# Experts of a two-layer block stack: the tokens' shift added on the vector engine, the gather issued a quad ahead, another order of the quads

## The chip, the core and the metric

The kernel runs on one core of one Trainium2 chip. A time is the device time of one execution in microseconds (us); of several runs the median is given. Its engines have their own instruction queues and run side by side: TensorE (PE; its weight loads are shown as PEld), the vector engine (DVE), ScalarE (ACT), GpSimd (POOL), and SyncE (SP), which here only issues transfers (DMA). Results of matmuls land in PSUM, all other tiles lie in SBUF.

## What is computed

A sequence of 256 tokens and a context of 256 tokens, each token a row of 1024 numbers, go through two layers and a few blocks behind them. Each layer has a mixer (attention and a convolution or pooling) and a mixture of 32 experts. Its input is normalised, then scaled and shifted by vectors that depend on the stream (one pair for the sequence, one for the context):

```python
h = _rmsnorm(x, gain) * (1 + scale) + shift        # scale, shift: one row of 1024 a stream

def _moe(h, grp_w, grp_b, exp_w, exp_b, w_gate, w_up, w_down):
    ...                      # a group of experts for each token, 2 experts in it, their weights
    def run(args):
        tok, wt, e = args
        xb = h_pad[tok]
        hid = jax.nn.silu(xb @ w_gate[e]) * (xb @ w_up[e])
        return (hid @ w_down[e]) * wt[:, None]
    ...                      # each token's two results are added up
```

A layer's experts hold 32 x 3 matrices of 1024 x 512 numbers in fp32, 201 MB. Layer 0 takes 512 tokens (both streams), layer 1 only the sequence's 256.

## The kernel before

The program runs eight stages one after the other: ab, moe0, cd, moe1 (the two layers), ar, mlp0, moba, mlp1. The change touches `moe`, which runs for layer 0 (four tiles of 128 tokens, two streams) and for layer 1 (two tiles, one stream).

**Weights.** The experts lie in eight quads of four. A quad has six units: two of gate weights, two of up, two of down. A unit is four transfers of 1024 KB on SP's queue (`experts`). Units go into a ring of three slots in layer 0 and four in layer 1, in the order in which they are used; `s.done(...)` behind a unit's last matmul frees its slot, and the next unit is issued into it. Each quad has a fixed number of blocks of 128 places for tokens, `BLOCKS`: in layer 0 quad 0 has two, quad 1 three, quads 2 to 4 two, quads 5 to 7 one; in layer 1 quad 1 has two and the others one. The quads run in the order `ORDER`, [0, 6, 1, 2, 3, 4, 5, 7].

**A quad.** `gather` builds a one-hot matrix OH (tokens by places) on the vector engine (L1150, L1151) and multiplies it with the tokens' rows, kept without their shift in two parts (mH, mL), so that the tokens of the quad stand in hg, transposed (L1533, L1534: 64 matmuls in layer 0, into banks of the PSUM tag `tp`, of which there are two). The shift comes in by a further product: four matmuls count for each place which stream it takes (L1528; ScalarE copies the result to `cnt`, L1529), and eight matmuls of four rows multiply that with the shift vectors (L1537). ScalarE copies a full bank to hg (L1539). The shift's rows are made earlier, by `shift_rows` within the router's stage: ScalarE copies at L1214 and L1215, vector engine at L1218. `quad` then multiplies hg with the gate and up units (L1570), 32 matmuls a unit and block; OH is transposed (L1579) and copied by ScalarE to OT (L1580); ScalarE takes silu of the gate part (L1584), the vector engine the product with the up part (L1585), TensorE transposes that (L1588), the vector engine copies it to hidT (L1589), and the down units follow (L1598). `split` cuts the result into two parts (ACT L1609, DVE L1610), and `add` multiplies them with OT, which brings them back to the tokens' rows (L1619, L1620; DVE L1622 and GpSimd L1624 add them to xs). The two halves of a quad's `add` are issued within the next quad, behind its first and its second gate unit.

**The order of the work.** Only the matmuls of a unit are kept in program order; what stands around them on TensorE is placed by a scheduler. The gathers of the second to sixth quad stand between the quad before and their own gate units, with pieces within the down units of the quad before.

**The general part.** Tokens that don't fit into a quad's blocks are handled by `leftover`, a branch and a loop that runs as many times as there are such groups; for these inputs it runs zero times. It stands behind the first `PART` = 6 quads. Ahead of it the last quad's `add` is done at once (the flush), behind it the remaining quads 5 and 7 run, gather first.

**Router weights.** Layer 1's (tile rtw, transfer issued by ScalarE in `router`, L1182) share a buffer with `cnt`, so they are fetched when cnt was used for the last time in layer 0, in quad 7.

Of the kernel before, what the change touches and what calls it, by code (L numbers as in the profile page):

```python
# [10 lines left out]
F32 = mybir.dt.float32  # L11
F32R = mybir.dt.float32r
# [3 lines left out]
OP = mybir.AluOpType  # L16
# [217 lines left out]
class K:  # L234
# [86 lines left out]
    def setup(s):  # L321
# [41 lines left out]

        s.sel = cp.tile([128, 2, 4, 4], F32, name="sel")
        ids = s.ident.rearrange("p (i c) -> p i c", i=4)
        for l in range(2):
            for o in (0, 2):
                nc.vector.tensor_copy(s.sel[:, l, :, o:o + 2], ids[:, :, 12 * l + 2:12 * l + 4])
        s.low = cp.tile([128, 1], F32, name="low")
        for o in (0, 64):  # L370
            nc.vector.tensor_scalar(s.low[o:o + 32], s.ip[:32, 0:1], 2.0, -1.0, op0=OP.is_ge, op1=OP.mult)
        s.ones = cp.tile([128, 128], F32, name="ones")
        nc.vector.memset(s.ones, 1.0)
        nc.vector.tensor_scalar(nsk, sk, -1.0, None, op0=OP.mult)
# [825 lines left out]
    def shift_rows(s, l, pool, pp):  # L1200


        nc, V = s.nc, s.nc.vector
        ps = pp.tile([128, 512], F32, name="sc", tag="sc", bufs=2)
        for i in range(4):
            o = 64 * (i // 2)
            nc.tensor.matmul(ps[o:o + 4, i % 2 * 256:(i % 2 + 1) * 256], s.sel[:, l, i], s.mods[1], start=True,
                             stop=True, skip_group_check=True)
        yield
        w = pool.tile([128, 512], F32, name="sw", tag="hw", bufs=4)  # L1210
        H = pool.tile([128, 512], F32R, name="swH", bufs=1)
        rows = [slice(o, o + 4) for o in (0, 64)]
        for o in rows:
            nc.scalar.activation(w[o], ps[o], AF.Copy)  # L1214
            nc.scalar.activation(H[o], ps[o], AF.Copy)  # L1215
        yield
        for o in rows:
            V.scalar_tensor_tensor(s.shift[o], H[o].bitcast(F32), s.low[o], w[o], op0=OP.mult, op1=OP.add)  # L1218

    def moe(s, l, tiles):  # L1220
# [4 lines left out]
        with ExitStack() as ctx:  # L1225
# [6 lines left out]
            s.shift = big.tile([68, 512], F32R, name="shift")  # L1232
# [5 lines left out]
            with tc.tile_pool(reuse_waits="tile", name="me_rt", bufs=3) as rp:  # L1238
# [6 lines left out]

                tk = rp.tile([128, 70], F32, name="tk", bufs=1)
                nc.gpsimd.memset(tk, 0.0)
                for o in (1, 3, 65, 67):
                    nc.gpsimd.memset(tk[:, o:o + 1], 1.0)
                s.take = big.tile([128, 70], F32R, name="take")  # L1250
                nc.gpsimd.tensor_copy(s.take, tk)

# [66 lines left out]
                with tc.manual_schedule(engines={mybir.EngineType.PE, mybir.EngineType.DVE}):  # L1319
                    shift = s.shift_rows(l, rp, pp)  # L1320
                    if nt > 2:
                        turn(0)
                        next(shift)
# [6 lines left out]
                        next(shift)  # L1330
                        square(3, False)
                        next(shift, None)
                    else:
                        next(shift)
                        next(shift)
# [3 lines left out]
                        next(shift, None)  # L1339
# [18 lines left out]
            base = np.cumsum([0] + blocks) * 128.0  # L1358

            for part in (range(s.PART), range(s.PART, 8)):  # L1360
                with tc.tile_pool(reuse_waits="tile", name="me_wk", bufs=1) as wk:
                    if part[0] == 0:
                        before = (rest, lambda: (s.table(pp, lx, s.ltab), s.slot_weights(nt, wk, pp, slot, wk_, wcol)))
                    for i in part:
                        q = s.ORDER[i]
                        got = first if i == 0 else s.gather(tiles, blocks[q], float(base[q]), qk, pp, hH, hL, slot)
                        split, add = s.quad(l, q, nt, blocks[q], int(base[q]), tiles, wk, qk, pp, g2, wcol, got, before)
                        tag = "tp" if i < 7 and max(blocks[q], blocks[s.ORDER[i + 1]]) > 2 else "sc"
                        before = (lambda: (add(0, tag), split(1)), lambda: add(1, tag))
                    if part[0] == 0:  # L1370
                        for f in before:
                            f()
                        before = (lambda: None,) * 2
                    else:
                        split(1)
                        for t in sorted(range(nt), key=lambda t: t < nt - 2):
                            for n in range(2):
                                add(n, ("tp", "sc")[n], (t,), True)
                if part[0] == 0:
                    with tc.tile_pool(reuse_waits="tile", name="me_lo", bufs=1) as wk:  # L1380
                        s.leftover(l, nt, tiles, wk, pp, hH, hL, g2, slot, wk_)
# [8 lines left out]
    PART = 6  # L1390
    ORDER = [0, 6, 1, 2, 3, 4, 5, 7]

    def leftover(s, l, nt, tiles, wk, pp, hH, hL, g2, slot, wt):
# [7 lines left out]
        with tc.If(n > 0), tc.For_i(0, n, 1) as it:  # L1401
# [27 lines left out]
            for t in range(nt):  # L1429
                o = 1 - tiles[t] // 2  # L1430
                mm(ps[:4, :32], s.take[:, o:o + 4].bitcast(F32), OH[:, t], start=t == 0, stop=t == nt - 1)
            cnt = wk.tile([4, 32], F32, name="lcnt")
            V.tensor_copy(cnt, ps[:4, :32])

            sh = wk.tile([4, 512], F32, name="lsh", tag="t", bufs=1)
# [967 lines left out]
```

## Time and profile before

| what | value |
|---|---|
| three runs | 2330.93 us median (2329.2 to 2331.31) |
| the profiled execution | 2333.8 us, its span 2331.8 us |
| TensorE busy in the span | 2060.5 us (88%) |
| vector engine, ScalarE, GpSimd busy | 1132.4, 796.7, 299.9 us |
| read from memory | 597 MB, 256 GB/s over the span |
| layer 0's experts | first gate matmul at 338.5, last scatter at 881.7 us |
| layer 1's experts | from about 1035 to about 1486 us |

Matmuls are pipelined: each lasts longer than the distance to the next, so the cost of a series is its busy time over its count or the distance between its first and last start. [...] "Idle before" a row is the time in which its engine did nothing ahead of it, and behind the arrow stands what ended that time.

### The profile page before, as it was taken

Reading aid. Unit: us, or ns where it says so; the run is one execution under the profiler, and the core shown is the slowest. Engines: PE = TensorE matmul, PEld = TensorE weight load, DVE = VectorE, ACT = ScalarE, POOL = GpSimd, SP = SyncE. Lnnn points to the kernel's source line nnn. Section 1 sums busy time; section 2 is a strip of 40 time slices with the busy share of each in tenths; the row PEclk is TensorE's granted clock in tenths of the full one; section 3 lists DMA queues with packets and bytes.
Section 4 is the critical chain, followed back from the end, with each engine's and each line's share of the span. In section 5 each row is a group of like instructions: output and inputs, shape, how many; then the busy total and the mean of one; then the engine's idle time right before and its main releaser. Section 6 shows DMA issues by size and latency. Waiting matters only on the chain. (4 is left out here: it accounts for less than half of the span.)

```text
span 2331.8 us, 33216 instructions
## 1 busy us (share of the span) xinstructions
PE 2060.5 (88%) x12749; PEld 1300.4 (56%) x12749; DVE 1132.4 (49%) x2315; ACT 796.7 (34%) x1595; POOL 299.9 (13%) x292
## 2 busy tenths in 40 slices
PE   5987989999998778988887776789999999999998
PEld 3763754434443336553322232587967887777886
DVE  4897582202222018561110111478857666877666
ACT  4353441101110006630000000365325555655555
POOL 1000020201102012010000000242101110021110
PEclk8998989999998799998998979897999999999999
DMA  9775519987998794359999999840024455434550
GB/s 347 298 289 172 189 55 398 423 340 309 378 376 356 298 392 183 127 220 424 424 424 425 424 392 424 358 163 10 1 109 177 153 190 196 152 118 167 190 189 36
DMA packets 95125, 600.34 MB, mean 257 GB/s; under 512 B 12912, under 2 KB 14064, under 8 KB 30448
## 3 DMA queue, kind: packets, MB, share of 16 engines
q1 hardware_dynamic: 88848, 589.34, 63.8%
q10 hardware_dynamic: 6112, 8.80, 1.1%
q8 instruction: 104, 1.70, 0.3%
q14 instruction: 61, 0.50, 0.1%
HBM read 597.05 MB, written 1.05 MB: 256 GB/s over the span
## 5 line engine op out<-in xcount | busy, mean ns | idle before, releaser
L414 DVE TENSOR_TENSOR L<-w,H 128x512 fp32r<-128x512 f32 (+1 forms) x520 | 368.3, 722 | 188.7 <-ACT H L413 178.7
L1570 PE MATMUL acc<-w,hg 128*32 128x512 f32 x2816 | 389.1, 618 | 49.9 <-DMA w<-exw 48.7
L413 ACT ACTIVATE H<-w 128x512 fp32r<-128x512 f32 (+1 forms) x528 | 324.6, 621 | 308.4 <-PE hid L1694 75.2
L1570 PEld LDWEIGHTS acc<-w,hg 128*32 128x32 f32 x2816 | 100.8, 113 | 292.6 <-issue 200.9
L1598 PE MATMUL acc<-w,hidT 128*32 128x512 f32 x1408 | 215.9, 642 | 49.9 <-DMA w<-exw 43.2
L1624 POOL TENSOR_TENSOR xs<-xs,yo 128x512 f32<-128x512 f32 x90 | 114.5, 1301 | 814.3 <-DVE yo L1622 814.0
L1694 PE MATMUL hid<-mh,H 128*128 128x512 f32 x512 | 185.1, 404 | 6.7 <-DVE mh L1643 5.4
L1585 DVE TENSOR_TENSOR sg<-acc,sg 128x512 f32<-128x512 f32 x22 | 15.2, 692 | 355.2 <-PE acc L1570 355.0
L1609 ACT ACTIVATE yH<-acc,kept 128x512 fp32r<-128x512 f32 x44 | 30.1, 688 | 418.5 <-PE acc L1598 359.8
L1610 DVE SCALAR_TENSOR_TENSOR yL<-acc,kept,yH 128x512 fp32r<-128x512 f32 x44 | 33.0, 749 | 279.6 <-ACT yH L1609 278.4
L1598 PEld LDWEIGHTS acc<-w,hidT 128*32 128x32 f32 x1408 | 51.6, 116 | 190.9 <-issue 99.9
L1695 PE MATMUL hid<-mh,L 128*128 128x256 f32 x512 | 145.2, 284 | 0.5 <-DVE L L414 0.5
L1533 PE MATMUL tp<-OH,mH 128*128 128x128 f32 (+2 forms) x384 | 111.2, 319 | 28.8 <-DVE OH L1151 12.3
L1694 PEld LDWEIGHTS hid<-mh,H 128*128 128x128 f32 x512 | 97.6, 191 | 32.8 <-ACT H L413 4.4
L1622 DVE TENSOR_TENSOR yo<-sc,g 128x512 f32<-128x512 f32 x74 | 49.6, 688 | 133.2 <-PE sc L1620 131.5
L1534 PE MATMUL tp<-OH,mL 128*128 128x128 f32 (+2 forms) x384 | 108.6, 311 | 0.0
L1533 PEld LDWEIGHTS tp<-OH,mH 128*128 128x128 f32 x384 | 82.9, 216 | 43.9 <-issue 29.1
L423 PE MATMUL pd<-L,uH 128*128 128x512 f32 x256 | 102.5, 400 | 1.1 <-DVE L L414 0.2
L1704 POOL TENSOR_TENSOR uL<-r,uH 128x256 fp32r<-128x256 f32 x64 | 59.2, 952 | 342.0 <-ACT uH L1703 254.8
L422 PE MATMUL pd<-H,uH 128*128 128x512 f32 x256 | 101.2, 395 | 0.0
L424 PE MATMUL pd<-H,uL 128*128 128x512 f32 x256 | 101.2, 395 | 0.0
L1695 PEld LDWEIGHTS hid<-mh,L 128*128 128x128 f32 x512 | 98.2, 192 | 1.6 <-DVE L L414 1.1
(716 smaller groups left out, 3898.6 us busy)
## 6 DMA issues: line engine op xcount, KB each, us to landing
w<-exw SPq DMA_DIRECT2D x384, 1024.0 KB, 16.4
w<-modw SPq DMA_DIRECT2D x96, 512.0 KB, 7.1
w<-up SPq DMA_DIRECT2D x32, 1024.0 KB, 4.9
w<-dn SPq DMA_DIRECT2D x32, 1024.0 KB, 4.7
w<-qkv SPq DMA_DIRECT2D x12, 1024.0 KB, 4.8
w<-pg SPq DMA_DIRECT2D x8, 1024.0 KB, 4.8
w<-ab_u SPq DMA_DIRECT2D x4, 1024.0 KB, 13.6
w<-ab_o SPq DMA_DIRECT2D x4, 1024.0 KB, 4.8
```

The lines of the kernel that those rows point to most:

```text
L413: nc.scalar.activation(H, w, AF.Copy)
L414: (nc.gpsimd if k % 8 in s.spread else nc.vector).tensor_sub(L, w, H.bitcast(F32))
L422: mm(o, a[0], b[0], start=start, stop=False)
L423: mm(o, a[0], b[1], start=False, stop=False)
L424: mm(o, a[1], b[0], start=False, stop=stop)
L1533: mm(got[k][1], hH[:, t, c], OH[:, t], start=t == 0 and k % n == 0, stop=False, skip_group_check=True)
L1534: mm(got[k][1], hL[:, t, c], OH[:, t], start=False, stop=False, skip_group_check=True)
L1570: mm(pg[m, a][32 * i:32 * i + 32, :], hg[:, 4 * hf + k, c:c + 32], u[:, i, k], start=hf == 0 and k == 0, stop=hf == 1 and k == 3, skip_gro ...
L1598: mm(py[n, a][32 * i:32 * i + 32, :], hT[:, a, 2 * hf + k, 32 * i:32 * i + 32], u[:, i, k, n * 512:(n + 1) * 512], start=hf == 0 and k == ...
L1624: (V if last and n else nc.gpsimd).tensor_add(xv, xv, tmp)
L1694: nc.tensor.matmul(ps[m], H[:, w], h[:, k], start=k == 0, stop=False, skip_group_check=True)
L1695: nc.tensor.matmul(ps[m][:, :256], L[:, w], h[:, k, :256], start=False, stop=k == 7, skip_group_check=True)
```

## The change

`shift_rows`, the count and the shift matmuls go. Instead `of_stream` multiplies a matrix of ones with OH, two matmuls for each stream, so that every partition has, for each place, how often the stream's tokens fill it; ScalarE copies that to `rows`. `shifted` then adds shift x rows to the gathered bank on the vector engine, once for each stream and 128 features: 16 instructions a gather in layer 0, which write hg. In layer 1, with one stream, ScalarE writes hg with the shift as a bias, eight instructions a gather. The next quad's `gather` is issued by the running one (`ahead`), between its up units and the transposes of its hid part; the whole loop over quads is in program order on TensorE; OT's transposes move ahead of the up units; hid is copied back into its own tile. `ORDER` becomes [0, 5, 1, 6, 2, 3, 4, 7] and `PART` 7, so that the general part's branch stands ahead of the last quad alone. The transfer of the router weights no longer waits for `cnt`.

```diff
+    def of_stream(s, pool, pp, tiles, OH, W, tag):
+        streams = sorted({t // 2 for t in tiles})
+        if len(streams) == 1:
+            return None
+        rows = pool.tile([128, 2, W], F32, name="rows", bufs=1)
+        one = s.ones if OH.dtype == F32 else s.onesr
+        for st in streams:
+            if st == 0 or 2 * W > 512:
+                ps = pp.tile([128, 512], F32, name=tag, tag=tag, bufs=2)
+            o = ps[:, st * W % 512 if 2 * W <= 512 else 0:][:, :W]
+            for u in range(2):
+                s.nc.tensor.matmul(o, one, OH[:, 2 * st + u], start=u == 0, stop=u == 1, skip_group_check=True)
+            s.nc.scalar.activation(rows[:, st], o, AF.Copy)
+        return rows
+
+    def shifted(s, out, x, rows, tiles, k):
+        mv = s.rt[0]
+        if rows is None:
+            st = tiles[0] // 2
+            s.nc.scalar.activation(out, x, AF.Identity, bias=mv[:, 0, st, k:k + 1])
+            return
+        for st in range(2):
+            s.nc.vector.scalar_tensor_tensor(out, rows[:, st], mv[:, 0, st, k:k + 1], out if st else x, op0=OP.mult, op1=OP.add)
...
-        OH = qk.tile([128, nt, W], F32R, name="OH", tag="ohs" if nb == 1 else "oh")
+        OH = qk.tile([128, nt, W], F32R, name="OH")
...
             for t in range(nt):
                 if count and t == nt - 1:
-                    ps = pp.tile([128, 512], F32, name="sc", tag="sc", bufs=2)
-                    for u in range(nt):
-                        o = 1 - tiles[u] // 2
-                        mm(ps[:68, :W], s.take[:, o:o + 68], OH[:, u], start=u == 0, stop=u == nt - 1)
-                    nc.scalar.activation(cnt, ps[:68, :W], AF.Copy)
+                    rows = s.of_stream(qk, pp, tiles, OH, W, "sc" if halves else "tp")
...
             for k in got:
-                h = slice(64 * (k // 4), 64 * (k // 4) + 4)
-                mm(got[k][1], s.shift[h, k % 4 * 128:(k % 4 + 1) * 128], cnt[h], start=False, stop=True, skip_group_check=True)
-                if k % n == n - 1:
-                    nc.scalar.activation(hg[:, k - n + 1:k + 1].rearrange("p k n -> p (k n)"), got[k][0][:, :n * W], AF.Copy)
+                s.shifted(hg[:, k], got[k], rows, tiles, k)
...
+        got = ahead() if ahead else None
+        for a in range(nb):
             ps = pp.tile([128, 512], F32, name="tp", tag="tp", bufs=2)
             for k in range(4):
-                nc.tensor.transpose(ps[:, k * 128:(k + 1) * 128], sg[:, k * 128:(k + 1) * 128], s.ident)
-            V.tensor_copy(hT[:, a].rearrange("p k n -> p (k n)"), ps)
+                nc.tensor.transpose(ps[:, k * 128:(k + 1) * 128], hid[a][:, k * 128:(k + 1) * 128], s.ident)
+
+            V.tensor_copy(hid[a], ps)
...
-    PART = 6
-    ORDER = [0, 6, 1, 2, 3, 4, 5, 7]
+    PART = 7
+    ORDER = [0, 5, 1, 6, 2, 3, 4, 7]
```

TensorE behind the branch of layer 0 before the change: L1533 and L1534 are the gather of quad 5, 64 matmuls of which the first three stand here.

```order
1512 L1401 REGISTER_ALU
1513 L1401 COMPARE_AND_BRANCH
1514 L1401 UNCONDITIONAL_BRANCH x2
1515 L1533 MATMUL tp<-OH,mH 128x128
1516 L1534 MATMUL tp<-OH,mL 128x128
1517 L1533 MATMUL tp<-OH,mH 128x128
```

The same place after it: L1540 are gate and up matmuls (quad 7's), L1550 OH's transposes, L1562 hid's, L1572 the down matmuls.

```order
1603 L1361 REGISTER_ALU
1604 L1361 COMPARE_AND_BRANCH
1605 L1361 UNCONDITIONAL_BRANCH x2
1606 L1540 MATMUL acc<-w_136,hg 32x512 x16
1607 L1540 MATMUL acc<-w_118,hg 32x512 x16
1608 L1550 MATMUL tp<-ident,OH 128x128 x4
1609 L1540 MATMUL acc<-w_127,hg 32x512 x16
1610 L1540 MATMUL acc<-w_136,hg 32x512 x16
1611 L1562 MATMUL tp<-ident,sg 128x128 x4
1612 L1572 MATMUL acc<-w_118,sg 32x512 x16
```

No gather stands between the branch and the gate matmuls any more.

TensorE in a quad of two blocks before the change, from its last gate unit on; the gather at the end (L1533) is the next quad's.

```order
1298 L1570 MATMUL acc<-w_133,hg 32x512 x32
1299 L1570 MATMUL acc<-w_142,hg 32x512 x2
1300 L1579 MATMUL tp<-ident,OH 128x128 x8
1301 L1570 MATMUL acc<-w_142,hg 32x512 x30
1302 L1588 MATMUL tp<-ident,sg 128x128 x8
1303 L1598 MATMUL acc<-w_124,hidT 32x512 x32
1304 L1598 MATMUL acc<-w_133,hidT 32x512 x32
1305 L1533 MATMUL tp<-OH,mH 128x256
```

The end of the next quad's gather (L1506, L1507) within such a quad after the change, and the vector engine's rows there, from the product with the up part (L1556) on.

```order
1419 L1506 MATMUL tp<-OH,mH 128x256
1420 L1507 MATMUL tp<-OH,mL 128x256
1421 L1562 MATMUL tp<-ident,sg 128x128 x8
1422 L1572 MATMUL acc<-w_118,sg 32x512 x32
1423 L1572 MATMUL acc<-w_127,sg 32x512 x32
1424 L1540 MATMUL acc<-w_136,hg 32x512 x32
```

```order
553 L1556 TENSOR_TENSOR sg<-acc,sg 128x512 x2
554 L1481 SCALAR_TENSOR_TENSOR hg<-rows,mv_2243,tp 128x256 x2
555 L1481 SCALAR_TENSOR_TENSOR hg<-rows,mv_2243,hg 128x256 x2
560 L1481 SCALAR_TENSOR_TENSOR hg<-rows,mv_2243,tp 128x256 x2
561 L1481 SCALAR_TENSOR_TENSOR hg<-rows,mv_2243,hg 128x256 x2
562 L1564 COPY sg<-tp 128x512 x2
```

The gather moved from behind the down matmuls to ahead of hid's transposes, and the next quad's gate matmuls follow the down matmuls directly; the copies of hid (L1564), for which the down matmuls wait, stand behind the vector engine's 16 shift instructions.

## Rows read from the trace of the kernel before

**Rows 1.** The page: GB/s in 40 slices of 58.3 us; transfers of weights.
```profile
GB/s 347 298 289 172 189 55 398 423 340 309 378 376 356 298 392 183 127 220 424 424 424 425 424 392 424 358 163 10 1 109 177 153 190 196 152 118 167 190 189 36
...
w<-exw SPq DMA_DIRECT2D x384, 1024.0 KB, 16.4
```

**Rows 2.** Stretches: length, busy PE PEld DVE ACT POOL, clock, DMA share, GB/s.
```profile
338.50:741.50 403.00, 393.29 (x3026) 176.51 (x3026) 90.22 (x199) 47.03 (x79) 57.20 (x46) 0.99 0.90 367
...
741.50:752.00 10.50, 0.03 (x1) 0.31 (x2) 0.75 (x2) 0.00 (x0) 3.13 (x3) 0.64 0.81 332
752.00:768.30 16.30, 16.30 (x76) 15.86 (x75) 0.00 (x0) 0.87 (x2) 0.00 (x0) 0.50 0.00 1
768.30:871.20 102.90, 77.98 (x469) 26.48 (x468) 11.17 (x22) 5.83 (x10) 10.27 (x9) 0.90 0.92 378
871.20:881.70 10.50, 9.91 (x42) 3.64 (x42) 4.78 (x8) 3.81 (x5) 2.88 (x2) 0.86 1.02 423
1049.00:1370.00 321.00, 252.65 (x1550) 90.90 (x1538) 43.57 (x77) 24.34 (x44) 30.11 (x24) 0.93 1.01 424
```

**Rows 3.** Timeline of TensorE at the branch: start, length, line, idle before.
```profile
741.10 0.40 PE L1620 MATMUL sc<-yL,OT 128*128 128x512 f32 x1
751.97 0.27 PE L1533 MATMUL tp<-OH,mH 128*128 128x128 f32 x1 [10.48 <-issue]
...
768.34 6.13 PE L1570 MATMUL acc<-w,hg 128*32 128x512 f32 x40
```

**Rows 4.** Groups on TensorE, 338 to 741 us: busy, mean ns, idle before.
```profile
L1570 PE MATMUL acc<-w,hg 128*32 128x512 f32 x1408 | 173.7, 594 | 0.6 <-ACT hg L1539 0.5
L1598 PE MATMUL acc<-w,hidT 128*32 128x512 f32 x704 | 84.5, 593 | 0.5 <-DVE hidT L1589 0.5
...
L1533 PE MATMUL tp<-OH,mH 128*128 128x256 f32 x112 | 29.7, 302 | 4.9 <-DVE OH L1151 4.9
...
L1537 PE MATMUL tp<-cnt,shift 4*128 4x256 f32 x29 | 7.5, 344 | 0.0
...
L1537 PE MATMUL tp<-cnt,shift 4*128 4x384 f32 x8 | 3.5, 435 | 0.0
...
L1537 PE MATMUL tp<-cnt,shift 4*128 4x128 f32 x8 | 1.3, 283 | 0.0
```

**Rows 5.** Timeline of TensorE: half a gather of one block; start of the flush.
```profile
396.49 0.33 PE L1533 MATMUL tp<-OH,mH 128*128 128x128 f32 x1
...
400.20 0.66 PE L1537 MATMUL tp<-cnt,shift 4*128 4x128 f32 x4
...
732.59 0.50 PE L1619 MATMUL sc<-yH,OT 128*128 128x512 f32 x1
```

**Rows 6.** Groups on the vector engine, 338 to 890 us.
```profile
L1610 DVE SCALAR_TENSOR_TENSOR yL<-acc,kept,yH 128x512 fp32r<-128x512 f32 x26 | 19.5, 750 | 135.0 <-ACT yH L1609 134.1
...
L1589 DVE COPY hidT<-tp 128x512 f32<-128x512 f32 x14 | 9.4, 689 | 5.0 <-PE tp L1588 5.0
...
L1151 DVE SCALAR_TENSOR_TENSOR OH<-i,sl,OH 128x256 fp32r<-128x256 f32 x16 | 7.0, 478 | 0.0
L1151 DVE SCALAR_TENSOR_TENSOR OH<-i,sl,OH 128x128 fp32r<-128x128 f32 x16 | 4.9, 345 | 0.0
```

**Rows 7.** Timeline of TensorE at two gathers; then the stretch behind the second.
```profile
531.21 0.36 PE L1533 MATMUL tp<-OH,mH 128*128 128x256 f32 x1 [1.30 <-DVE OH L1151]
...
599.53 0.36 PE L1533 MATMUL tp<-OH,mH 128*128 128x256 f32 x1 [1.80 <-DVE OH L1151]
...
600.00:608.00 8.00, 8.00 (x40) 7.16 (x38) 3.36 (x14) 0.98 (x2) 0.00 (x0) 0.57 1.01 422
```

**Rows 8.** Waits of SP's queue, 741 to 890 us: total, times, longest.
```profile
SPq L281 <- DMA rtw<-rtw: 15.1, 1, 15.1
```

**Rows 9.** Timeline of ScalarE in layer 1's router.
```profile
1006.35 0.59 ACT L1214 ACTIVATE sw<-sc 4x512 f32<-4x512 f32 x1 [3.56 <-DVE wo L996]
...
1009.76 1.57 ACT L1263 ACTIVATE hT<-acc,mv 128x256 f32<-128x256 f32 x4
```

More of the change, by code (lines that the diff above doesn't have):

```diff
@@ L362, in setup @@
             nc.vector.memset(s.eps[:, j:j + 1], s.EPSS[j])
[L364 to L371, printed above, removed]
         s.ones = cp.tile([128, 128], F32, name="ones")
         nc.vector.memset(s.ones, 1.0)
+        s.onesr = cp.tile([128, 128], F32R, name="onesr")
+        nc.vector.tensor_copy(s.onesr, s.ones)
         nc.vector.tensor_scalar(nsk, sk, -1.0, None, op0=OP.mult)
@@ L1198, in router @@
         s.rt = mv, rtw, bl
-    def shift_rows(s, l, pool, pp):
-        nc, V = s.nc, s.nc.vector
-        ps = pp.tile([128, 512], F32, name="sc", tag="sc", bufs=2)
[L1205 to L1218, printed above, removed]
     def moe(s, l, tiles):
@@ L1244, in moe @@
                 mv, rtw, bl = s.rt
[L1246 to L1251, printed above, removed]
                 def turn(j0):
@@ L1358, in moe @@
             base = np.cumsum([0] + blocks) * 128.0
-            for part in (range(s.PART), range(s.PART, 8)):
-                with tc.tile_pool(reuse_waits="tile", name="me_wk", bufs=1) as wk:
-                    if part[0] == 0:
[L1363 to L1381, printed above, removed]
@@ new lines, in moe @@
+            ahead = [lambda q=q: s.gather(tiles, blocks[q], float(base[q]), qk, pp, hH, hL, slot) for q in s.ORDER[1:]]
+            got = first
+            with tc.manual_schedule(engines={mybir.EngineType.PE}):
+                for part in (range(s.PART), range(s.PART, 8)):
+                    with tc.tile_pool(reuse_waits="tile", name="me_wk", bufs=1) as wk:
+                        if part[0] == 0:
+                            before = (rest, lambda: (s.table(pp, lx, s.ltab), s.slot_weights(nt, wk, pp, slot, wk_, wcol)))
+                        for i in part:
+                            q = s.ORDER[i]
+                            split, add, got = s.quad(l, q, nt, blocks[q], int(base[q]), tiles, wk, qk, pp, g2, wcol, got, before,
+                                                     ahead[i] if i < 7 else None)
+                            tag = "tp" if i < 7 and max(blocks[q], blocks[s.ORDER[i + 1]]) > 2 else "sc"
+                            before = (lambda: (add(0, tag), split(1)), lambda: add(1, tag))
+                        if part[0] == 0:
+                            for f in before:
+                                f()
+                            before = (lambda: None,) * 2
+                        else:
+                            split(1)
+                            for t in sorted(range(nt), key=lambda t: t < nt - 2):
+                                for n in range(2):
+                                    add(n, ("tp", "sc")[n], (t,), True)
+                    if part[0] == 0:
+                        with tc.tile_pool(reuse_waits="tile", name="me_lo", bufs=1) as wk:
+                            s.leftover(l, nt, tiles, wk, pp, hH, hL, g2, slot, wk_)
@@ L1514, in gather @@
         n = 4 // nb
-        cnt = s.cq.tile([68, W], F32R, name="cnt", tag="rtw")
+        rows = None
         def part(k0, k1, count):
+            nonlocal rows
             got = {}
@@ L1546, in gather, with quad @@
         return OH, hg
-    def quad(s, l, q, nt, nb, base, tiles, wk, qk, pp, g2, wcol, gathered, before):
-        nc, tc, V, mm = s.nc, s.tc, s.nc.vector, s.nc.tensor.matmul
+    def quad(s, l, q, nt, nb, base, tiles, wk, qk, pp, g2, wcol, gathered, before, ahead):
+        nc, V, mm = s.nc, s.nc.vector, s.nc.tensor.matmul
         T = nt * 128
```

82 lines of the change are left out of this document (32 added, 50 removed).

## The prediction

> **What bounds the kernel now.** I read the 40 slices first [rows 1]: a slice is 58.3 us, so the seventh to the fifteenth (398 to 392 GB/s) are layer 0's experts, where the transfers move 298 to 423 GB/s, and the nineteenth to the twenty-fifth (424 in all but one) are layer 1's. A unit of expert weights is four transfers of 1024 KB [rows 1]; at 424 GB/s that is 4.194 MB / 424 = 9.9 us, and a layer has 48 of them.
>
> The table by stage [rows 2] cuts layer 0's experts at the flush (741.5), the branch (752), the gather behind it (768.3), the last transfer (871.2) and the end (881.7). Up to the flush TensorE is busy 393.29 of 403 us: TensorE itself is the bound there, and the transfers, at 367 GB/s, have some slack. From 741.5 it is idle for 10.48 us, and no engine or transfer releases it, only issue [rows 3]: that is the branch of the general part, whose loop runs zero times. [...] From 768.3 on TensorE waits for weights (busy 77.98 of 102.9). So layer 0 has a stretch bound by TensorE, then some 20 us in which the transfers do nothing, then a stretch bound by the transfers. Layer 1's experts are bound by the transfers throughout: 424 GB/s with TensorE busy 252.65 of 321 [rows 2].
>
> **Part 1: after the branch.** Before, 881.7 - 741.5 = 140.2 us. 12 units are used there, three lie in the ring, nine are fetched: 9 x 9.9 = 89, and 10.5 + 16.3 + some 4 (until the first slot is freed) + 89 + 10.5 (from the last transfer to the end) make 130; the missing 10 are the first landing, transfers for the next phase on the same queue, and a stall of SP that waited 15.1 us for the router weights' transfer [rows 8]. After the change only quad 7 is left, and its gather lies ahead of the branch: 10.5 for the branch, its first gate unit 7.9 (32 matmuls of 173.7 / 1408 = 0.123 us [rows 4], twice that at the lower clock), 3 units x 9.9 = 29.7, a share of those 10 of 4 (between 1 and 8), and the same 10.5 behind. Sum 62.6; **-78 us**. The ring still stands full during the branch and the first unit (the transfers ran on at 332 GB/s through most of the branch [rows 2], so the hole is some 10 us instead of 20); that is in the sum. The router weights of layer 1 are now issued behind the squares of the first router, so SP's 15.1 us cannot recur; its cost is among the 10.
>
> **Part 2: before the branch,** where every us of TensorE counts. Added: quad 5, one block wide. Gate and up 128 x 0.123 = 15.8, down 64 x (84.5 / 704 = 0.120) = 7.7 [rows 4]; gather 64 matmuls, of which 32 took 400.20 - 396.49 = 3.7, so 7.4; scatter 16 of the 32 in the flush, which ran 732.59 to 741.5, so 4.5; eight transposes at the gather's 0.12 each, 1 [rows 5]. Sum 36.4. Quad 7's gather with its ones matmuls: 7.9. The four ones matmuls stand for the four count matmuls, at no cost. Removed: the shift matmuls, 7.5 + 3.5 + 1.3 = 12.3, and the gathers' waits for their one-hot, 4.9 [rows 4], because the gather now comes two units after its one-hot can be built. Net +27.1.
>
> New waits on TensorE, once for each of seven gathers (quads 5, 1, 6, 2, 3, 4, 7). No row shows the new vector operation, which reads PSUM and two broadcast rows. The nearest are the vector engine's scalar_tensor_tensor: 0.478 us at 256 columns, 0.345 at 128, from SBUF, and 0.750 at 512 from PSUM [rows 6]. The slope is about 0.27 us per 256 columns, so 512 from PSUM comes down to 0.48 at 256. I take 0.345, 0.48 and 0.61 for one, two and three blocks; the upper end is 0.75 for all. The 16 of a gather then last 5.5, 7.7 and 9.8 us, beside a gather of 7.4 to 11.3. These are about equal, so the vector engine ends behind TensorE, not far behind.
>
> What follows: the rows' round trip through ScalarE costs 0.8 a gather (it waits twice for a copy, where before it waited for none), 5.6. The hid copies (0.69 each [rows 6]) stand behind all 16 operations on the vector engine and the down matmuls behind those, where before the down matmuls waited 0.5 us in all for such copies [rows 4]: 2 a gather, 14 (between 7 and 35). One-hots that are built too late in the narrow quads 5 and 6, where only two units of 3.9 us lie between, 4. After the two-block quads the next gate unit is done before the halves that the vector engine splits, and the next gate bank waits for it: 5 (0 to 7). Quad 1's wider scatter behind GpSimd's additions, 3. Two more stretches at the lower clock than now, 5. Sum 36.6; **+64 us** in all, so that the flush ends near 805 (741.5 + 64). Transfers set no bound there: 39 units x 9.9 are 386 us of the 466 between 338.5 and 805.
>
> [...]
>
> **Part 3: routers and layer 1.** In layer 0 ScalarE's four shift copies go from between the squares (about 2 us), but eight of the new operations come into the vector engine's chain of routing: net +1 (-2 to +3). In layer 1 those copies run from 1006.35 to 1009.76 ahead of what the router's transposes wait for [rows 9], of which about 2.5 lie on the path: **-2.5**. Its gathers keep ScalarE for the shift (now a bias), in eight small copies for two; with TensorE idle for a fifth of the time, and the transfers at 424 GB/s, that cost is hidden behind the transfers: 0. Were the cover gone, six more small instructions, at the nearest row's 0.345 us [rows 6], would be 2 us in each of eight quads.
>
> Sum: -78 + 64 + 1 - 2.5 = -15.5 on the profiled 2333.8 (span 2331.8 and 2 around it). The median of the runs is 2.9 lower, 2330.9; so **about 2315**.
>
> **The rivals.** (a) *The new waits hide.* The two engines overlap well, TensorE's idle time is half of my 36.6: 18 less, **2297**. For it: the vector engine is busy only 90.22 of 403 us there [rows 2]. Against: in the new order TensorE has nothing to issue behind the gather but what waits for the vector engine.
>
> (b) *Each wait lowers the clock.* After the gap of 1.80 us that ends at 599.53 the window 600 to 608 shows 0.57 [rows 7], some 3.4 us lost; behind the 10.5 us gap the clock stood at 0.50 [rows 2]. If every one of seven gathers ends in such a stretch, 7 x 3.4 = 24 instead of my 5, part of it given back as fewer waits for weights: +16, **2331**, no change. For it: seven new gaps of about 3 us, longer than the one that lowered it. Against: the gap of 1.30 us at 531 did not lower it, since the stage's mean of 0.99 [rows 2] leaves room for 8 us at the lower level and the 8 us at 600 take 7 of them. [...]
>
> (c) *Slower: the vector engine becomes the bound of every gather.* At 0.75 us, the row from PSUM, 16 operations last 12 us where a gather has 7.4; over my mean of 0.44 that is 0.31 x 16 x 7 = +35, **2350**. It decides from +21, that is from about 0.63 us an operation, or 3 us more idle for each gather. Against: 128 and 256 columns have never cost that.
>
> (d) *It does not do what it says:* the gather of quad 7 would stay behind the branch. The new order of TensorE has the gate matmuls as its first rows after the branch, so I give it no chance.
>
> **How the numbers follow.** Forecast (2304 to 2326) 0.50, (a) 0.23, (b) 0.17, (c) 0.10. What a measurement can tell from no change is about 0.2%, 4.7 us: 2326.3 to 2335.6. Faster: 0.50 + 0.23 and a quarter of (b), 0.77; same: the rest of (b), 0.13; slower: (c), 0.10. The range leaves out (c) and the far half of (a): 2294 to 2334.
>
> **What would show it.** Right: flush ends at 795 to 815; from there to the end of layer 0's experts some 62 us, with a transfer hole of about 10 us instead of 20; L1540 as the first matmul after the branch; TensorE idle for 2 to 4 us before each L1562 or L1572, released by the vector engine; L1481 at 0.35 to 0.6 us; the clock's row with two or three stretches below 1 ahead of the branch. Layer 1's experts as long as now. Wrong: L1481 at 0.63 or more (c); a clock below 0.95 over the whole stretch before the branch (b); idle time before L1562 and L1572 under 1.5 us each (a); a stretch after the flush of 75 us or more would show that my 10 us of overhead do not shrink with the units.

## The result and the profile after

The changed kernel takes 2300.01 us in the median of four runs (2296.35 to 2304.11), the kernel before 2330.06; the ratio is 0.9875 (95% interval 0.985 to 0.9901), some 29 us less. The profiled execution took 2304.11 us, its span is 2302.0. The forecast was 2315, its range 2294 to 2334: the sign and the range hold, but the gain is almost twice the 16 us that the sum gave.

The stretches of layer 0's experts, cut as in [rows 2] at the flush's end, the return of the transfers, the last transfer and the last scatter; then layer 1 (length; busy us of PE, PEld, DVE, ACT, POOL; clock as the granted share of TensorE's full clock, of which 0.50 is the lower of the two levels in these records; DMA share, GB/s):

```profile
335.60:793.15 457.55, 426.34 (x3334) 194.65 (x3334) 159.29 (x364) 37.70 (x67) 67.76 (x55) 0.98 0.92 381
793.15:805.80 12.65, 6.50 (x44) 1.95 (x48) 0.75 (x2) 0.00 (x0) 3.10 (x3) 0.73 0.48 194
805.80:838.20 32.40, 22.14 (x134) 5.60 (x126) 1.38 (x2) 1.08 (x2) 0.00 (x0) 0.88 0.99 413
838.20:850.23 12.03, 11.32 (x42) 4.19 (x42) 4.85 (x8) 4.96 (x7) 2.97 (x2) 0.76 1.02 417
1040.00:1370.00 330.00, 256.39 (x1502) 81.01 (x1501) 49.33 (x76) 27.41 (x66) 30.05 (x24) 0.91 1.01 421
```

Beside [rows 2], the stretch ahead of the branch has grown from 403.0 to 457.6 us, and what lies behind the flush has shrunk from 140.2 to 12.65 + 32.40 + 12.03 = 57.1. The stretch without transfers, 16.3 us at 1 GB/s before, is now a part of the 12.65 us, in which they still move 194 GB/s: they stand, at 9 GB/s, for 6.5 us, from 799.30 to 805.80. Layer 1 runs at 421 GB/s where 424 stood: small, but it covers 460 us.

TensorE behind the branch, beside [rows 3] (start, length, idle before it):

```profile
799.30 8.93 PE L1540 MATMUL acc<-w,hg 128*32 128x512 f32 x64 [6.15 <-PEq L1361]
808.16 0.66 PE L1550 MATMUL tp<-ident,OH 128*128 128x128 f32 x4
808.75 4.49 PE L1540 MATMUL acc<-w,hg 128*32 128x512 f32 x36
```

The gate matmuls follow the branch directly. TensorE is idle for 6.15 us, not 10.48, and the first two units take 8.93 us together, since the clock was at its lower level for part of them only (0.50 from 799.30 to 803.10, 1.00 from there to 808.20).

Which waits TensorE has ahead of the branch (total us, times, longest), to be held against the 4.9 us for one-hots in [rows 4]:

```profile
PE acc L1540 <- DMA w<-exw: 10.8, 9, 2.0
PE acc L1572 <- DVE sg L1564: 5.2, 6, 1.9
PE tp L1562 <- DVE hg L1481: 4.9, 5, 1.3
PE tp L1469 <- ACT rows L1470: 3.3, 7, 0.6
PE acc L1540 <- DVE hg L1481: 2.1, 2, 1.6
PE tp L1550 <- ACT OT L1551: 2.1, 1, 2.1
```

The one-hot's wait is gone. The waits for the vector engine's shift operations and the copies behind them come to 5.2 + 4.9 + 2.1 = 12.2 us, and the longest item is one that I had left out: weights.

The vector engine's shift operations, beside [rows 6] (busy us, mean ns, idle before):

```profile
L1481 DVE SCALAR_TENSOR_TENSOR hg<-rows,mv,hg 128x256 f32<-128x256 f32 x32 | 14.0, 478 | 0.0
L1481 DVE SCALAR_TENSOR_TENSOR hg<-rows,mv,tp 128x256 f32<-128x256 f32 x32 | 13.9, 476 | 12.2 <-PE tp L1507 12.2
...
L1481 DVE SCALAR_TENSOR_TENSOR hg<-rows,mv,tp 128x128 f32<-128x128 f32 x24 | 7.2, 342 | 16.0 <-PE tp L1507 16.0
...
L1481 DVE SCALAR_TENSOR_TENSOR hg<-rows,mv,tp 128x384 f32<-128x384 f32 x8 | 4.9, 614 | 3.8 <-PE tp L1507 3.0
```

They cost what the nearest rows gave, 0.34, 0.48 and 0.61 us. The vector engine waits for TensorE, 31 us in all, more than TensorE waits for it. One gather of two blocks shows how they run side by side (the vector engine, start and length):

```profile
700.12 0.87 DVE L1481 SCALAR_TENSOR_TENSOR hg<-rows,mv,tp 128x256 f32<-128x256 f32 x2 [2.52 <-PE tp L1507]
...
702.23 0.87 DVE L1481 SCALAR_TENSOR_TENSOR hg<-rows,mv,tp 128x256 f32<-128x256 f32 x2 [0.44 <-PE tp L1507]
...
706.07 0.87 DVE L1481 SCALAR_TENSOR_TENSOR hg<-rows,mv,tp 128x256 f32<-128x256 f32 x2 [0.26 <-PE tp L1507]
706.86 0.87 DVE L1481 SCALAR_TENSOR_TENSOR hg<-rows,mv,hg 128x256 f32<-128x256 f32 x2
707.65 1.28 DVE L1564 COPY sg<-tp 128x512 f32<-128x512 f32 x2
```

and TensorE's end of it:

```profile
705.87 0.60 PE L1562 MATMUL tp<-ident,sg 128*128 128x128 f32 x4
707.00 0.66 PE L1562 MATMUL tp<-ident,sg 128*128 128x128 f32 x4 [0.53 <-DVE hg L1481]
708.39 4.07 PE L1572 MATMUL acc<-w,sg 128*32 128x512 f32 x36 [0.73 <-DVE sg L1564]
```

The vector engine follows bank by bank with gaps of 0.26 to 0.44 us; only the last bank's four operations and the copies lie behind the gather, and TensorE loses 0.53 + 0.73 us, not 2.

### The profile page after: what moved, and what is told of

Same layout as the page of the kernel before. It is cut to its first block, busy times and chain, and to the rows that moved or that the text cites. A ratio compares the mean times of both kernels' runs of the same rounds, so it can differ in the third digit from the quotient of the medians.

```text
span 2302.0 us, 33046 instructions
## 1 busy us (share of the span) xinstructions
PE 2024.8 (88%) x12589; PEld 1267.2 (55%) x12589; DVE 1195.0 (52%) x2434; ACT 782.9 (34%) x1603; POOL 298.6 (13%) x280
## 5 line engine op out<-in xcount | busy, mean ns | idle before, releaser
L1540 PE MATMUL acc<-w,hg 128*32 128x512 f32 x2816 | 426.7, 652 | 98.4 <-DMA w<-exw 76.4
L1540 PEld LDWEIGHTS acc<-w,hg 128*32 128x32 f32 x2816 | 103.0, 118 | 390.2 <-issue 225.3
L1572 PE MATMUL acc<-w,sg 128*32 128x512 f32 x1408 | 187.5, 621 | 38.9 <-DMA w<-exw 27.3
L1556 DVE TENSOR_TENSOR sg<-acc,sg 128x512 f32<-128x512 f32 x22 | 15.2, 691 | 245.0 <-PE acc L1540 245.0
L1572 PEld LDWEIGHTS acc<-w,sg 128*32 128x32 f32 x1408 | 48.6, 113 | 163.8 <-issue 98.9
L1506 PE MATMUL tp<-OH,mH 128*128 128x128 f32 (+2 forms) x384 | 96.6, 291 | 0.3 <-ACT rows L1470 0.2
L1555 ACT ACTIVATE sg<-acc 128x512 f32<-128x512 f32 x22 | 13.1, 600 | 245.4 <-PE acc L1540 147.5
L1507 PE MATMUL tp<-OH,mL 128*128 128x128 f32 (+2 forms) x384 | 94.5, 286 | 0.0
```

The lines of the kernel that those rows point to most:

```text
L1506: mm(got[k], hH[:, t, c], OH[:, t], start=t == 0 and k % n == 0, stop=False, skip_group_check=True)
L1507: mm(got[k], hL[:, t, c], OH[:, t], start=False, stop=t == nt - 1, skip_group_check=True)
L1540: mm(pg[m, a][32 * i:32 * i + 32, :], hg[:, 4 * hf + k, c:c + 32], u[:, i, k], start=hf == 0 and k == 0, stop=hf == 1 and k == 3, skip_gro ...
L1572: mm(py[n, a][32 * i:32 * i + 32, :], hid[a][:, (2 * hf + k) * 128 + 32 * i:(2 * hf + k) * 128 + 32 * i + 32], u[:, i, k, n * 512:(n + 1) ...
```

## The experiments

In the table, "ahead" is the length from layer 0's first gate matmul to the flush's end, "behind" from there to its last scatter, "layer 1" from its first gate matmul to its last scatter, each from the timeline of TensorE in the one profile of that kernel. Repeats of the same kernel differ by up to 3.4 us in a stage (before: 140.2 and 136.8 us behind the flush). Ratios are to the kernel before, timed beside it.

| kernel | ahead | behind | layer 1 | ratio (95% interval) |
|---|---|---|---|---|
| before_again | 403.0 | 136.8 | 455.7 | |
| after (the first profile) | 457.5 | 57.1 | 460.8 | 0.9875 (0.985 to 0.9901) |
| after_again | 458.8 | 54.1 | 459.9 | 0.9854 (0.9825 to 0.9882) |
| old_order | 457.0 | 62.9 | 460.3 | 0.9868 (0.9841 to 0.9896) |
| branch_earlier | 406.3 | 119.4 | 462.6 | 0.9891 (0.9863 to 0.9919) |
| gather_behind_down | 452.6 | 55.2 | 461.0 | 0.9818 (0.98 to 0.9836) |
| shift_by_matmul | 450.5 | 56.0 | 453.5 | 0.9836 (0.9822 to 0.985) |
| vector_16_more | 480.9 | 54.1 | 458.5 | 0.9975 (0.9961 to 0.9988) |
| hid_within_gather | 470.8 | 57.0 | 461.0 | 0.993 (0.9908 to 0.9952) |
| aligned_ring | 457.2 | 55.1 | 451.6 | 0.9824 (0.9808 to 0.984) |
| before_aligned | 400.1 | 135.9 | 454.2 | 0.9953 (0.9939 to 0.9967) |
| matmul_shift_aligned | 449.9 | 55.9 | 454.1 | 0.9826 (0.9809 to 0.9844) |
| branch_last | 496.3 in all | | 452.7 | 0.9856 (0.9841 to 0.9871) |

**The two kernels once more, on one chip.** 

> The changed kernel unchanged, on the chip on which the kernel before is run beside it. Two theories on layer 1's experts, which took 460.8 us from the first gate matmul to the last scatter against 455.8 before: (1) the transfers of that execution ran a little slower (421 instead of 424 GB/s), which belongs to the execution and not to the kernel: then before and after show the same GB/s in layer 1 here, and the stage's lengths differ by under 2 us. (2) The new order costs layer 1 some 5 us: then the difference stays, at equal GB/s. Time for both: ratio to before 0.984 to 0.991.

> The kernel before, for its trace on the same chip. Under (1) layer 1's experts take within 2 us of what the changed kernel takes here; under (2) some 5 us less. Flush end near 741, 140 us from there to the end of layer 0's experts.

Layer 1's difference stays, 459.9 against 455.7, and so does that of the transfers, first row before, second after:

```profile
1040.00:1370.00 330.00, 264.78 (x1607) 95.35 (x1606) 43.63 (x78) 26.47 (x47) 30.18 (x24) 0.89 1.01 424
```

```profile
1040.00:1370.00 330.00, 253.39 (x1520) 86.07 (x1518) 48.72 (x75) 28.13 (x70) 27.52 (x22) 0.93 1.01 421
```

So (1) falls; but (2) said "at equal GB/s", and that falls too: the transfers themselves are slower. In the records of the single packets of 8 KB in this stretch, the mean is 311.6 ns before and 314.0 after; before, one of four units in turn took 315 and the others 309 to 311, and after, all took 314. With four slots in the ring, that points to the slots.

**The slots' addresses.** The change adds a tile of ones and drops two small ones ahead of the ring, which moves all slots by 352 bytes. The run puts two unused tiles ahead of them:

```diff
+        s.pad = cp.tile([128, 48], F32, name="pad")
+        nc.vector.memset(s.pad, 0.0)
...
+        if l == 0:
+            s.pad2 = s.cq.tile([128, 56], F32, name="pad2", tag="pad2")
+            nc.gpsimd.memset(s.pad2, 0.0)
```

> The changed kernel with two unused tiles ahead of the ring's slots, so that all four slots of the weights begin at multiples of 256 bytes within a partition (before the change two of four did; after it none). Open: layer 1's experts take 4 to 5 us longer than in the kernel before, at 421 instead of 424 GB/s, in every run. Theory A, the slots' addresses, which the change moved by 352 bytes: then packets in layer 1 fall from 314 to about 309 ns, the transfers run at 424 GB/s or a little above, and layer 1's experts take 455 us or less instead of 460; in all 4 to 7 us faster than the changed kernel. Theory B, the new order of work in layer 1 disturbs the transfers: then nothing changes, within 2 us.

Theory A holds: with every slot at a multiple of 256 bytes, packets take 309.5 ns in all four slots and layer 1's row is

```profile
1040.00:1370.00 330.00, 248.93 (x1562) 85.00 (x1562) 49.70 (x76) 29.64 (x74) 27.99 (x23) 0.97 1.01 427
```

Layer 1's experts take 451.6 us, 8 less than in the changed kernel and 4 less than in the kernel before.

> The kernel before with two unused tiles ahead of the ring's slots, so that all four slots begin at multiples of 256 bytes in a partition (two of four do in the kernel before). If the address alone sets the speed of the transfers: packets in layer 1 of 309 to 310 ns in all four slots, 427 GB/s, layer 1's experts 451 to 452 us instead of 455.7, and the rest as before: 3 to 6 us faster than the kernel before. If the gain of the run with aligned slots came from the two together: no change.

The same in the kernel before (where, beside the two tiles, a small one of the loop that runs zero times shares a buffer): 309.6 ns, 426 GB/s, and a ratio of 0.9953, 11 us. Its profile shows 1.5 us of that in layer 1 and 3 ahead of the branch; but the profiled execution was its slowest, 2331.26 us for a median of 2321.25, so the profile can't size the gain, and where the rest lies stays open. That moving the slots alone speeds the transfers is shown; how much time it gives is better seen in the changed kernel.

**The order and the branch.**

```diff
-    ORDER = [0, 5, 1, 6, 2, 3, 4, 7]
+    ORDER = [0, 6, 1, 2, 3, 4, 5, 7]
```

> The changed kernel with the old order of the quads, 0, 6, 1, 2, 3, 4, 5, 7, and the branch still ahead of quad 7. Theory: what counts is that one quad and not two lies behind the branch; the order only decides where TensorE waits for weights, so the time is within 4 us of the changed kernel. Rival: the one-block quads stand between wide ones so that the ring can fill again; with quads 4 and 5 side by side the waits for weights grow, 8 us or more slower.

Ahead of the branch the old order costs nothing (457.0), behind it 8.7 us more. The transfers there:

```profile
796.30:859.20 62.90, 43.83 (x217) 11.67 (x216) 7.47 (x13) 6.05 (x9) 7.59 (x6) 0.78 0.96 393
```

393 GB/s over 62.9 us are 5.9 units; after_again's 54.2 us at 364 GB/s are 4.7. With quads 4 and 5 side by side, one more unit is still to be fetched at the flush. So the ring does fill less, as the rival says, but it shows behind the branch: ahead of it TensorE's waits for weights are 10.1 us, not more than after_again's 11.6. The clock behind it is lower too (0.78 for 0.87), and how the 8.7 us divide between the two isn't separated. In time the run is 6 us slower by medians, and the intervals overlap.

> The changed kernel with the old order and the branch ahead of quads 5 and 7, as before; the gathers stay a quad ahead and the shift on the vector engine. Theory: behind the branch there are six more units to fetch, 59 us, of which some 37 us were saved ahead of it, so the time is 10 to 20 us above the changed kernel, and still 10 to 20 below the kernel before. Rival: the gain came from the gather that no longer stands alone behind the branch; then it is within 5 us of the changed kernel.

```profile
339.80:746.10 406.30, 382.77 (x3050) 176.38 (x3050) 142.37 (x328) 34.78 (x61) 57.57 (x47) 0.99 0.89 367
746.10:865.50 119.40, 87.58 (x501) 29.80 (x500) 21.20 (x48) 8.04 (x14) 15.99 (x13) 0.90 0.94 387
```

12 us above the changed kernel, as expected, and 24 below the kernel before, where 10 to 20 were. The early gather, with what else changed within a quad (the shift on the vector engine, the program order on TensorE), takes 17.4 us from behind the branch (136.8 to 119.4) for 3.3 more ahead of it. The branch stands at its old place here, and TensorE is idle at it for 5.7 us, as in the changed kernel, and not for the 10.6 of before_again: the shorter pause doesn't come from its place; why it is shorter isn't shown. Layer 0's experts take 539.8 us before, 525.7 here, 519.8 with the old order and one quad behind the branch, 512.9 as changed.

**The shift.** The matmuls, the count and the router's copies of the kernel before, put into the changed one:

```diff
-                s.shifted(hg[:, k], got[k], rows, tiles, k)
+                h = slice(64 * (k // 4), 64 * (k // 4) + 4)
+                mm(got[k], s.shift[h, k % 4 * 128:(k % 4 + 1) * 128], cnt[h], start=False, stop=True, skip_group_check=True)
+                if k % n == n - 1:
+                    nc.scalar.activation(hg[:, k - n + 1:k + 1].rearrange("p k n -> p (k n)"), bank[k][:, :n * W], AF.Copy)
```

> The changed kernel with the shift as before: made in the router's stage, counted and added by matmuls of four rows, ScalarE copying the banks; order, early gather and branch as changed. Theory: for seven gathers the shift matmuls cost TensorE some 14 us again and the router's copies 3 in each layer, while the waits for the vector engine (12.7 us ahead of the branch) shrink to those for ScalarE's copies, some 5: 0 to 8 us slower than the changed kernel. Rival: the shift on the vector engine is what brings the gain: 15 us or more slower. Its slots lie at the addresses of the kernel before, modulo 256, so under theory A of the run with aligned slots layer 1 shows 424 GB/s, which takes 3 us off.

The rival falls: it is no slower. The theory, with the 3 us for the addresses, left -3 to +5 us; the ratios say 4 us faster, with overlapping intervals. TensorE's waits ahead of the branch fall to

```profile
PE acc L1592 <- DMA w<-exw: 8.7, 9, 1.5
...
PE tp L1602 <- ACT OT L1603: 2.1, 1, 2.1
PE acc L1624 <- DVE sg L1616: 1.6, 2, 0.8
PE acc L1592 <- ACT hg L1561: 0.9, 2, 0.5
```

and the stretch is 8.3 us shorter than after_again's, although TensorE is busier (434.9 for 427.4 us). Between the layers 3.8 us are lost (148.7 us for 144.9), most of it not by the router's copies (see part 3 below). Layer 1 is 6.5 us shorter; the slots' addresses explain some 4 of that, the difference between the two kernels above, and the rest is open. Without the addresses the two ways are about equal.

```diff
-        for st in range(2):
+        for st in (0, 0, 0, 1):
```

> The changed kernel with each gather's first shift operations done three times (16 more vector instructions a gather in layer 0, the same output). Theory (the term of the sum): the vector engine ends behind TensorE already, so that nearly each added us lies on the path: 3 x 5.5 + 3 x 7.7 + 9.8 = 49 us ahead of the branch, some 12 of them given back as fewer waits for weights: 35 to 49 us slower than the changed kernel. Rival: the vector engine's work is hidden beside the gather: under 15 us slower.

Neither: 22.1 us more ahead of the branch (28 by the ratios). Its row there is

```profile
339.50:820.40 480.90, 432.90 (x3334) 194.24 (x3334) 204.96 (x488) 37.71 (x67) 67.73 (x55) 0.97 0.88 362
```

so the vector engine is busy 45.5 us more than in after_again (159.45), where 49 were estimated. TensorE's waits for the vector engine rise from 12.7 (after_again, a smaller one included) to

```profile
PE tp L1506 <- DVE hg L1481: 11.2, 10, 1.5
PE tp L1562 <- DVE sg L1564: 8.1, 6, 2.3
...
PE tp L1562 <- DVE hg L1481: 6.5, 6, 1.2
PE acc L1540 <- DVE hg L1481: 4.8, 2, 2.5
PE acc L1572 <- DVE sg L1564: 4.1, 2, 2.3
```

34.7 us, while the waits for weights fall from 11.6 to 7.2. TensorE is also busy 5.5 us more (427.39 in after_again), at a mean clock of 0.97 for 0.98. So some half of the added work still lies beside the gather: as changed, the vector engine has room there.

**The gather's place.**

```diff
-        got = ahead() if ahead else None
         for a in range(nb):
...
+        got = ahead() if ahead else None
         split(0)
```

> The changed kernel with the next quad's gather issued behind the running quad's down matmuls instead of ahead of hid's transposes; shift, order and branch as changed. Theory: the place of the gather within the quad decides little: the waits behind it only change their place (the next gate matmuls then wait for the vector engine's last shift operations, 2 to 3 us a gather, as the down matmuls do now for the copies of hid), and hid's transposes wait about 1.3 us a quad for silu and product: 3 to 12 us slower than the changed kernel. Rival: it is the early gather that lets TensorE work on: 20 us or more slower, near the kernel before.

It is 6 us faster ahead of the branch, against both. The 12.2 us of waits for shift and copies come down to

```profile
PE tp L1561 <- DVE sg L1556: 2.8, 6, 1.0
...
PE acc L1540 <- DVE hg L1481: 2.1, 2, 1.6
...
PE acc L1571 <- DVE sg L1563: 1.6, 2, 0.8
```

The first of these is a new wait, for the product with the up part, as the theory had it, but 2.8 us in six waits and not 1.3 a quad. The 2.1 us are quad 0's; no other quad's gate matmuls wait for the vector engine. That they begin with the first features, which are done by then, is the likely reason. By the ratios it is 8 us, and the intervals overlap a little.

Moving hid's transposes instead (`turned`, called by the gather behind its fourth feature block):

```diff
+            if mid and k + n == 4:
+                mid()
...
+        got = ahead(turned) if ahead else None
```

> The changed kernel with hid's transposes and copies issued in the middle of the next quad's gather instead of behind it, so that the down matmuls no longer wait for the vector engine's 16 shift operations. Theory: the waits ahead of L1562 and L1572 (4.9 + 5.2 us in the profile) go, and part returns as waits for weights and for PSUM banks: 3 to 10 us faster. Rival: the banks of the gather's second half then wait for the copies, so that the waits only move: within 3 us or slower.

Slower, by 12 us ahead of the branch. The down matmuls' 5.2 us of waits for the copies are gone; hid's transposes still wait 5.1 us for shift operations, and the gather's second half now waits 2.2 for the copies, so the rival's mechanism is there too. But the loss is not in the waits: TensorE is busy 12.3 us more, at a lower mean clock:

```profile
337.60:808.40 470.80, 439.72 (x3334) 203.03 (x3334) 159.29 (x364) 37.82 (x67) 67.69 (x55) 0.96 0.90 370
```

A mean of 0.96 over 470.8 us is 38 us at the lower level, against 18 at 0.98 in after_again; half of the difference, some 10 us, is lost. The clock's own records give 41.0 us against 17.1, in five stretches in either kernel, so 12 us. Why the clock stayed low for longer here isn't settled.

**Put together.** shift_by_matmul with aligned slots and, in layer 1, ScalarE's bias:

> The changed kernel with aligned slots, the shift by matmul in layer 0 (as before the change) and by ScalarE's bias in layer 1 (as changed). The sum of what the runs showed: from the run with aligned slots, 8 us less ahead of the branch, 2 more behind it: 2283 to 2288 us, some 11 to 16 below the changed kernel. If the gain of the shift by matmul came from elsewhere (its slots' addresses), no better than the run with aligned slots, 2291.

2288.69 us, a ratio of 0.9826: the 7 us ahead of the branch are there (449.9 for aligned_ring's 457.2), but 3.4 us are lost between the layers (147.3 for 143.9; see part 3 below) and 2.5 in layer 1, for a cause left open, and in time it is not to be told from aligned_ring or gather_behind_down. The medians of all three are below those of both kernels of this study; against the changed kernel, their intervals overlap after_again's and not that of the first measurement.

```diff
-                for part in (range(s.PART), range(s.PART, 8)):
+                for part in (range(s.PART), range(s.PART, 8)) if nt == 2 else (range(8),):
...
```

> The kernel of the run matmul_shift_aligned with the general part's branch behind all eight quads in layer 0 (layer 1 as changed). Theory: one flush of 9 us, the stretch at the lower clock and the hole in the transfers go, while the branch itself (6 us of TensorE) moves to the end of the layer: 5 to 10 us faster than that run. Rival: at the end the branch costs more than in the middle, since the next phase's first transfers and its first work then wait for it: no faster, or slower.

The rival: layer 0's eight quads end after 496.3 us instead of 505.7, but then the branch stands between the layers, ahead of work that has nothing beside it:

```profile
840.13 0.69 PE L502 MATMUL tp<-ident,mods 128*128 128x128 f32 x2 [6.17 <-DVEq L1408]
853.74 3.75 PE L530 MATMUL tp<-ident,xn 128*128 128x128 f32 x16 [9.51 <-DVE xn L527]
```

From layer 0's last scatter to layer 1's first gate matmul it takes 167.6 us instead of 147.3. Of the 20 us, 8 are lost up to the second of these rows (the wait in it was 6.4 us in matmul_shift_aligned); behind it TensorE's mean clock is lower as well (0.84 over the whole stretch, for 0.90), and the rest is not taken apart. In the middle, the transfers run on during the branch: 389 GB/s from 793.15 to 799.30 in the changed kernel, 185 here from 833.96 to 840.13.

## Why the prediction was right, and where its sizes were off

**What bounds the kernel, and where the gain is:** right. It came from the stretch behind the flush, where the branch and quad 5's gather had left the transfers without a free slot: 1 GB/s for the gather's 16.3 us [rows 2].

**Part 1, -78 us:** measured -83.1. The branch cost 6.15 us of TensorE instead of 10.5, the first unit some 5 instead of 7.9 because the clock came back after 3.8 us of it; the last stretch was 12.0 instead of 10.5. The 9.9 us a unit and the 4 us of overhead held (32.4 us from the transfers' return to the last one). The hole in the transfers was 6.5 us, not 10.

**Part 2, +64 us:** measured +54.6 (+55.8 on one chip). TensorE's busy time grew by 33.0 us, where the work of the sum (36.4 + 7.9 - 12.3) and 5 for the clock gave 37: right. The clock's share is right too: the stretches of the lower level ahead of the branch are

```profile
410.00:435.00 25.00, 20.83 (x104) 8.88 (x103) 11.47 (x26) 2.07 (x4) 5.07 (x4) 0.86 1.01 420
...
485.00:510.00 25.00, 25.00 (x216) 9.00 (x215) 4.17 (x12) 0.87 (x2) 0.00 (x0) 0.93 0.76 301
510.00:535.00 25.00, 22.82 (x192) 11.09 (x194) 6.23 (x19) 0.56 (x2) 0.00 (x0) 0.93 0.46 185
...
585.00:610.00 25.00, 19.92 (x132) 5.43 (x129) 4.15 (x6) 1.38 (x2) 3.63 (x3) 0.93 1.01 420
```

0.14 + 3 x 0.07 of 25 us, 8.8 us lost where the kernel before lost 3.4 [rows 7]. The step that failed is the term of the new waits. Its parts: the rows' round trip 3.5 for 5.6; the copies behind the shift operations, with the bank they wait for, 10.1 for 14; the late one-hots and the next gate bank, 9 together, not there; quad 1's scatter, 3, hardly there (TensorE's waits for the scatter's vector operations are 1.9 us, and were 1.5 before), and a wait for OT of 2.1 in its place. Against that, "transfers set no bound there" was wrong: 11.5 us of waits for weights, most of them in the one-block quads, which use a unit in less than 4 us while one takes 9.9. A total over the whole stretch (386 of 466 us) can't show that. In all, engines' waits were about half of what I took, and TensorE's waits ahead of L1562 and L1572 some 1 us each (4.9 us in 5, 5.2 in 6) and not 2 to 4, which is rival (a) in its mechanism. That its time, 2297, is near the 2300 measured is in part luck: of the 18 us by which (a) lies below the sum, part 2 gave 9, since weights took back what the engines' waits left; part 1 gave 5 more and layer 0's start 4, and layer 1's experts took 5.

**Part 3:** for the router of layer 1 the sum had -2.5; the stretch between the layers measured -2.9 (-3.8 on one chip), but that is luck. The gain lies at the stretch's other end, ahead of the next stage's first transposes. ScalarE's first square behind layer 0, and these transposes, before the change:

```profile
887.03 1.06 ACT L404 ACTIVATE junk<-xs 128x1024 bf16<-128x1024 f32 x1 [7.62 <-PE sc L513]
...
893.46 3.77 PE L527 MATMUL tp<-ident,xn 128*128 128x128 f32 x16 [6.44 <-DVE xn L524]
```

and after it:

```profile
849.04 1.06 ACT L397 ACTIVATE junk<-xs 128x1024 bf16<-128x1024 f32 x1 [1.12 <-PE tp L1593]
...
858.66 3.77 PE L520 MATMUL tp<-ident,xn 128*128 128x128 f32 x16 [2.17 <-DVE xn L517]
```

Before, the squares wait for TensorE's L513, and the transposes begin 11.7 us behind the last scatter (881.73); after, 8.4 us behind it (850.23). From there to layer 1's first gate matmul it takes 137.0 us before and 137.4 after (136.5 in after_again), so the term that was forecast doesn't show. shift_by_matmul and matmul_shift_aligned begin those transposes at 11.7 us too, and behind them they take 137.0 and 135.6 us, with the router's copies in layer 1 and without: the copies are worth 1.5 us at most. aligned_ring takes 135.5 there, so the 3.4 us that matmul_shift_aligned lost between the layers are these as well. Why ScalarE waits there in the kernels with the shift by matmul isn't shown. Layer 0's start, +1, came out at -2.9 and -0.5, and lies between 334.7 and 339.8 us in the profiles of the kernels that share it; one profile can't size it. Layer 1's experts, 0, measured +5.0 and +4.2: wrong, and by a cause that none of the rows read ahead of it shows, the slots' new addresses.

**The rivals.** (b) fell: four stretches of the lower clock, one as long as the old one (6.8 us from 420.8 on; before, 6.8 from 601.0) and three half as long (3.4 us each, from 485.7, 519.8 and 594.9 on), not seven of the old length. (c) fell by its price, 0.75 us, and vector_16_more shows its weight was too large as well: there about half of the added vector work reached the time. At 256 columns 0.476 us were measured from PSUM and 0.478 from SBUF. The narrower of these operations cost more for a column: 0.342 us at 128 columns are 2.7 ns each, 0.614 at 384 are 1.6.

**The parts of the change.** What won in layer 0 is the gather ahead of the branch (14.1 us, with what else changed within a quad), one quad alone behind the branch (5.9) and the order (6.9); the last two, in the runs' times, have intervals that overlap. The gather's place within the quad cost 6 us against a place behind the down matmuls, in one profile, and the shift on the vector engine brought nothing that these runs can tell. The program order on TensorE, the earlier transposes of OT, hid's copy into its own tile and the router weights' transfer were not tried apart.

## What to carry to other kernels

Where a branch or any other pause stands between work on a full ring, put ahead of it whatever frees no slot, and leave behind it as few transfers as can be: here that was worth 83 us behind the branch for 55 ahead of it. Two engines that handed over bank by bank cost each other here little more than the last bank (0.53 + 0.73 us in the gather shown above), so price a new wait by its tail and not by the difference of the totals; and look for a bound by transfers quad by quad. Where a term of a sum comes out right in the length of a stage, check in the timeline that the gain lies where the term put it. After any change that adds or drops a tile, compare the transfers' GB/s (here 421 with the slots moved by 352 bytes, for 424) before the order of work is blamed.

## What the runs showed of the hardware

Not expected: here the place in SBUF at which a transfer landed set its speed. The addresses here follow from the sizes of the tiles ahead of the slots. Between 1040 and 1370 us, packets of 8 KB took 309.5 ns on average with all four slots at multiples of 256 bytes (aligned_ring) and 314.0 with all four 64 or 96 bytes behind such a multiple (after_again): 427 against 421 GB/s, or 8 us of layer 1's 460. In the kernel before, with two slots at such multiples and two 224 bytes behind one, a single slot took 315 and the others 309 to 311, so the distance from a multiple is not all that counts; other steps than 256 bytes were not tried. These runs moved the side that is written; why an address costs time is not shown.
